# Two-layer decoder trunk on one core: order of the first loads, flags fetched one by one, later mixture weights, a second buffer of unsplit columns

## The chip, the core and the metric

The kernel runs on one core of a Trainium2 chip. The metric is the device time of one execution in microseconds (us), the median of several runs. The core's engines are TensorE (PE, its weight loads PEld), VectorE (DVE), ScalarE (ACT), GpSimd (POOL) and SyncE (SP). Each takes its own instructions in order; semaphores order them against each other. SP and ACT issue DMAs, and 16 DMA engines carry them.

## What is computed

A trunk of two layers on 256 tokens of width 1024, all in float32. Each layer is a token mixer and a feed-forward part, both with RMS norm, and both shifted, scaled and gated by columns that come from a vector c through a matrix ("ada"). The feed-forward part of layer 0 is dense, that of layer 1 a mixture of 8 experts, two for each token. Cut to what matters:

```python
mod = silu(c) @ ada_w[l] + ada_b[l]           # 6 x 1024: shift, scale, gate, twice
h = rms_norm(x, norm_mix[l]) * (1 + scale) + shift
x = x + gate * hybrid_mixer(h, ...)           # gated DeltaNet and stick-breaking attention
h = rms_norm(x, norm_ffn[l]) * (1 + scale2) + shift2
x = x + gate2 * (swiglu(h) if l == 0 else moe_swiglu(h))
# moe_swiglu: logits = h @ router_w + router_b; the two largest of 8; softmax over the two;
#   y_e = (silu(xb @ w1[e]) * (xb @ w3[e])) @ w2[e]; summed with the mixture weights
out = rms_norm(x, final_norm)
```

The width of an expert's hidden layer is 3584.

## The kernel before

**Stages.** Four stages follow each other: mixer 0 (to about 366 us, the program's start included), the dense feed-forward part (to 640), mixer 1 (to 996) and the experts (to 1965). Weights come from HBM in units of 1 MB on SP's queue. A unit is split into a high part (`CAST hl` on ACT) and a low part (`lo`, a subtraction on DVE), and a product is made of three matmuls of parts.

**Program start.** `ada_first` loads eight 1 MB units of ada_w (tiles `f`), makes silu(c) (tile `csil`, a column of 128 partitions by 8, loaded element by element, L145), spreads it (L235) and multiplies (L252). `setup(0)` loads five small tensors of rows on ACT's queue into the tile `rows` (L174 to L178), and PE turns them into columns (L183). `load_rows` loads the first constants `cst` (L157, the identity for transposes among them) and x (L158). The router's bias and matrix (`rb`, `rw`, L1112, L1113) and `setup(1)`'s five loads have no place of their own in the program: a scheduler puts them where their operands are free, which is on ACT's queue in these first 20 us. Each DMA reports to one of eight semaphores, taken in turn; a DMA waits for the landing of the one that had its semaphore before.

**Experts.** `route` finds each token's two experts, its slot with each, and the mixture weights `wt`. `Light` sets a flag for each expert with at most 64 tokens (`light`, `lighti`) and loads the eight flags into registers of PE (L1207, TENSOR_LOAD). By the flag a branch (`arms`) takes one of two ways for each pair of units: `few` multiplies the unsplit weights (L1372 up, L1454 down), `heavy` the parts (L1351 up, L1438 and L1443 down). `gather` builds selection matrices `pe` (L1214, L1215, L1296) and gathers two experts' tokens with 32 matmuls (L1314), whose columns ACT and DVE split (L1325, L1330, L1331). The experts' hidden layer is worked off in blocks of 1024 columns; `down` of a block runs after the next block's `up`. `turned` transposes the hidden columns (L1412) and copies them, split (`t2r`, L1416, L1417) and unsplit (`s`, L1420; one buffer, `s32`). `begin(e)` makes, at an expert's start, its mixture weights by slot (`ws`, L1393, L1402) and the matrix `pte` (L1398, L1400) that puts its rows back; `finish` uses both (L1488, L1493, L1494).

**Order.** A scheduler places instructions by priority and readiness; a DMA marked with `keep_in_program_order`, as those of the experts' weights on SP are, stays where the program has it.

Of the kernel before, what the change touches and what calls it, by code (L numbers as in the profile page):

```python
# [11 lines left out]
F32 = mybir.dt.float32  # L12
# [7 lines left out]
P = 128  # L20
# [53 lines left out]
def trunk_kernel(  # L74
# [17 lines left out]
    phase_b = dict(raw2=4, hl2=1, lo=4, r4=6, x32=3, s32=1, t2=5, t2r=6, gt=1, xn=2, pe=2, pte=2)  # L92
# [77 lines left out]
    def setup(l):  # L170

        rows = pc.tile([P, 2, P], F32, tag="rows", name=f"rows{l}")
        G.memset(rows, 0.0)
        nc.scalar.dma_start(rows[0:48, 0, :], ada_b[l].rearrange("(r p) -> r p", p=P))  # L174
        nc.scalar.dma_start(rows[48:56, 0, :], norm_mix[l].rearrange("(r p) -> r p", p=P))
        nc.scalar.dma_start(rows[56:64, 0, :], norm_ffn[l].rearrange("(r p) -> r p", p=P))
        nc.scalar.dma_start(rows[64:65, 0, :], dn_out_norm[l : l + 1, :])
        nc.scalar.dma_start(rows[0:96, 1, :], conv_w[l].rearrange("j (r p) -> (j r) p", p=P))  # L178
# [53 lines left out]
    def ada_first(l, mods):  # L232

        cs = mk("r4", [P, 4 * S])[:, : 32 * KC].rearrange("p (k c) -> p k c", c=32)
        V.tensor_copy(cs, csil.unsqueeze(2).broadcast_to([P, KC, 32]))  # L235
        banks = {m: [bank(t) for _ in range(2)] for m, t in zip(mods, "gs")}
        raws = {}
        for m in mods:
            for q in range(4):
                raws[m, q] = ada_load(l, m, q, "f8")  # L240
                if len(raws) == 2:
                    load_rows()
                if len(raws) == 5:
                    rest = setup(0)
        for m in mods:
# [862 lines left out]
    class Router:  # L1108


        def __init__(self, l, j):
            nc.scalar.dma_start(rb, router_b[j : j + 1, :].partition_broadcast(P))  # L1112
            nc.scalar.dma_start(rw[:, 0], router_w[j].rearrange("(k p) n -> p k n", p=P))  # L1113
# [44 lines left out]
    def route():  # L1158
# [21 lines left out]
        wgt = sm([P, 2, 2])  # L1180
        V.tensor_sub(wgt, m8[:, :, 0:2], m8[:, :, 0:1].broadcast_to([P, 2, 2]))
        A.activation(wgt, wgt, AF.Exp)
        den = sm([P, 2])
        V.tensor_reduce(den, wgt, AX.X, ALU.add)
        V.reciprocal(den, den)
        V.tensor_tensor(wgt, wgt, den.unsqueeze(2).broadcast_to([P, 2, 2]), ALU.mult)
        V.tensor_tensor(wt, eq, wgt[:, :, 0:1].broadcast_to([P, 2, NE]), ALU.mult)
        V.tensor_tensor(tmp, tmp, wgt[:, :, 1:2].broadcast_to([P, 2, NE]), ALU.mult)
        V.tensor_add(wt, wt, tmp)
        return oa, wt, pos, light  # L1190

    zero = pc.tile([P, P], F32R, tag="zero", name="zero")
    most = pc.tile([P, 1], F32, tag="most", name="most")
    mosti = pc.tile([P, 1], I32, tag="mosti", name="mosti")

    class Light:


        def __init__(self, cnt):
# [4 lines left out]
            self.back = pc.tile([P, NE], F32, tag="back", name="back")  # L1204
            V.tensor_scalar(self.back, self.flag, -float(P // 2), None, ALU.mult)
            self.regs = [
                nc.values_load(self.int[0:1, e : e + 1], engines=[mybir.EngineType.PE], min_val=0, max_val=1)  # L1207
                for e in range(NE)
            ]

        def slots(self, e):

            t = mk("t2", [P, 512])[:, 0:P]
            V.tensor_scalar(t, C["iota"], P // 2 - 0.5, self.back[:, e : e + 1], ALU.is_gt, ALU.mult)  # L1214
            V.tensor_add(t, t, C["iota"])  # L1215
            return t

# [6 lines left out]
    class Weights:  # L1224
# [53 lines left out]
        def group(self):  # L1278
# [5 lines left out]
    def experts(l, weights, xnh, xnl, oa, wt, pos, light, merge):  # L1284
# [50 lines left out]
        def up(e, n):  # L1335
# [8 lines left out]
            def heavy(u0, units):  # L1344
                for u, (_, hv, lv) in enumerate(units):
# [326 lines left out]
```

## Time and profile before

| | us |
|---|---|
| median of 3 runs | 1971.96 (1966.64 to 1973.22) |
| the profiled execution, its own time | 1972.13 |
| its span | 1970.3 |
| PE busy | 1823.6 (93%) |
| DVE busy | 1599.0 (81%) |
| ACT busy | 1283.3 (65%) |

The mean granted clock of TensorE was 0.965. The span runs from the first to the last recorded instruction; 1.8 us of the profiled execution's time lie around it. The chain of work that ended last is made of TensorE for 63%, DVE for 18%, ACT for 8% and DMA for 4%. In a timeline a row is one instruction or a run of alike ones: its start, its length, the engine, the line, what it writes and reads, and in brackets how long the engine was idle before it and what ended that. An engine with a q behind its name is its sequencer, which issues DMAs.

### The profile page before, as it was taken

The numbers are of one execution on the slowest core, as the hardware profiler recorded it, in microseconds if no ns is written. First come the engines' busy times: TensorE is split into PE (matmuls) and PEld (weight loads), VectorE is DVE, ScalarE is ACT, GpSimd is POOL, SyncE is SP. The second block draws the span as 40 slices with busy tenths as digits, with TensorE's granted clock in tenths as the row PEclk, the third lists the DMA queues.
The fourth block names the chain that finished last, engine by engine and source line by source line (L and its number), as shares of the span: only waits on it lengthen the run. The fifth ranks groups of instructions, "written<-read, shape, count | busy, mean of one in ns | idle before, by whom it ended". The sixth has DMA issues, their size and how long they took to land.

```text
span 1970.3 us, 36475 instructions
## 1 busy us (share of the span) xinstructions
PE 1823.6 (93%) x14868; PEld 1412.8 (72%) x14868; DVE 1599.0 (81%) x1900; ACT 1283.3 (65%) x1842; POOL 80.0 (4%) x88
## 2 busy tenths in 40 slices
PE   5899999999999899999979988999889998899986
PEld 2889989999999789989968733686337863378522
DVE  3778678687666878588668898997989889898998
ACT  2765556454443665556477788877788687886885
POOL 0101000000000101000000002000020001000000
PEclk8999999999999999999989999999899998899998
DMA  8544447688773344555739999999999999999995
GB/s 279 168 155 144 143 153 235 214 288 279 246 260 95 127 153 131 162 171 193 259 140 377 365 402 348 380 369 365 381 355 383 367 370 365 370 374 368 377 403 232
DMA packets 220334, 539.24 MB, mean 274 GB/s; under 512 B 13602, under 2 KB 120548, under 8 KB 206052
## 3 DMA queue, kind: packets, MB, share of 16 engines
q1 hardware_dynamic: 215216, 536.02, 74.7%
q8 instruction: 148, 2.42, 0.5%
q10 hardware_dynamic: 4916, 0.35, 0.2%
q14 instruction: 54, 0.44, 0.1%
HBM read 535.27 MB, written 1.06 MB: 272 GB/s over the span
## 4 chain that ended last, share of the span: by engine, by line
PE 63%; DVE 18%; ACT 8%; issue 7%; DMA 4%; DVEq 0%; SPq 0%; ACTq 0%
PE g L1351 15%; PE g L379 7%; PE g L375 7%; PE g L377 7%; DVE lo L1271 7%; PE a L1438 4%; PE g L1372 3%; ACT hl L1267 3%; DMA raw<-in_moe_w_dram 2%; PE a L1454 2%; PE a L1443 2%; DVE t L627 2%; DVE hl L340 2%; ACT hl L339 1%; PE a L1055 1%
## 5 line engine op out<-in xcount | busy, mean ns | idle before, releaser
L1271 DVE TENSOR_TENSOR lo<-raw,hl 128x2048 fp32r<-128x2048 f32 (+1 forms) x338 | 754.1, 2272 | 46.5 <-ACT hl L1267 46.4
L1267 ACT CAST hl<-raw 128x1024 fp32r<-128x1024 f32 x672 | 657.3, 1052 | 26.0 <-DMA raw<-in_moe_w_dram 21.6
L340 DVE TENSOR_TENSOR hl<-raw,hl 128x1024 fp32r<-128x1024 f32 (+1 forms) x252 | 298.1, 1188 | 136.8 <-ACT hl L339 136.4
L339 ACT CAST hl<-raw 128x1024 fp32r<-128x1024 f32 (+1 forms) x252 | 256.8, 1022 | 201.3 <-PE g L379 134.0
L375 PE MATMUL g<-r,hl 128*128 128x256 f32 x1536 | 235.2, 293 | 6.6 <-ACT r L483 3.4
L377 PE MATMUL g<-r,hl 128*128 128x256 f32 x1536 | 228.6, 288 | 0.0
L379 PE MATMUL g<-r,hl 128*128 128x256 f32 x1536 | 223.9, 287 | 0.4 <-DVE hl L340 0.4
L1351 PE MATMUL g<-hl,r 128*128 128x512 f32 x896 | 222.9, 391 | 0.0
L375 PEld LDWEIGHTS g<-r,hl 128*128 128x128 f32 x1536 | 204.2, 194 | 15.2 <-ACT r L483 4.7
L1372 PE MATMUL g<-raw,x 128*64 128x512 f32 (+1 forms) x1024 | 212.1, 563 | 0.0
L377 PEld LDWEIGHTS g<-r,hl 128*128 128x128 f32 x1536 | 204.6, 195 | 3.0 <-issue 2.5
L379 PEld LDWEIGHTS g<-r,hl 128*128 128x128 f32 x1536 | 202.6, 194 | 2.6 <-issue 1.9
L1351 PEld LDWEIGHTS g<-hl,r 128*128 128x128 f32 x896 | 167.4, 188 | 37.0 <-ACT hl L1267 2.4
L1372 PEld LDWEIGHTS g<-raw,x 128*64 128x64 f32 x1024 | 71.5, 141 | 114.6 <-issue 104.2
L1454 PE MATMUL a<-raw,s 128*64 128x512 f32 x448 | 120.2, 684 | 3.6 <-ACT s L1420 3.2
L1351 PE MATMUL g<-lo,r 128*128 128x512 f32 x448 | 120.7, 391 | 0.5
L1416 ACT CAST t2r<-a 128x512 fp32r<-128x512 f32 x56 | 32.8, 585 | 113.1 <-PE a L1412 113.1
L1351 PEld LDWEIGHTS g<-lo,r 128*128 128x128 f32 x448 | 83.6, 188 | 20.0 <-DVE lo L1271 2.9
L210 DVE SCALAR_TENSOR_TENSOR f<-raw,csil,f 128x1024 f32<-128x1024 f32 x70 | 92.5, 1322 | 5.7 <-DMA raw<-in_ada_w_dram 5.2
L1438 PE MATMUL a<-hl,t2r 128*128 128x512 f32 x224 | 89.0, 397 | 1.7 <-ACT hl L1267 1.7
L1454 PEld LDWEIGHTS a<-raw,s 128*64 128x64 f32 x448 | 34.3, 157 | 74.5 <-issue 67.3
L1443 PE MATMUL a<-hl,t2r 128*128 128x512 f32 x224 | 87.5, 390 | 0.0
(334 smaller groups left out, 2211.6 us busy)
## 6 DMA issues: line engine op xcount, KB each, us to landing
raw<-in_moe_w_dram SPq DMA_DIRECT2D x334, 1024.0 KB, 7.0
raw<-in_w_in_dram SPq DMA_DIRECT2D x60, 1024.0 KB, 5.4
raw<-in_ffn_w_dram SPq DMA_DIRECT2D x42, 1024.0 KB, 5.8
raw<-in_ada_w_dram SPq DMA_DIRECT2D x40, 1024.0 KB, 5.3
f<-in_ada_w_dram SPq DMA_DIRECT2D x8, 1024.0 KB, 8.6
raw<-in_w_up_dn_dram SPq DMA_DIRECT2D x8, 1024.0 KB, 5.1
raw<-in_w_out_dram SPq DMA_DIRECT2D x8, 1024.0 KB, 5.0
raw<-in_w_up_sb_dram SPq DMA_DIRECT2D x4, 1024.0 KB, 5.1
```

The costliest lines, as they stand in the source:

```text
L339: A.copy(hv, part)
L340: V.tensor_sub(lv, part, hv.bitcast(F32))
L375: T.matmul(pv[:, b, :], hv[:, k, :], xh[:, k, :], start=(k == 0), stop=False)
L377: T.matmul(pv[:, b, :], hv[:, k, :], xl[:, k, :], start=False, stop=False)
L379: T.matmul(pv[:, b, :], lv[:, k, :], xh[:, k, :], start=False, stop=(k == kc - 1))
L1267: A.copy(hi[:, h, :], raw[:, h, :])
L1271: V.tensor_sub(lo[:, h, :], raw[:, h, :], hi[:, h, :].bitcast(F32))
L1351: T.matmul(ps, x_[:, kk, :], w[:, k, 512 * b : 512 * b + 512], start=(kk == 0 and x_ is xh and w is hv), stop=(kk == KC - 1 and w is lv),)
L1372: T.matmul(banks[0][h, 0:half], x32[:, kk, :], w[:, k, half * i : half * i + half], start=(wide and kk == 0), stop=(kk == KC - 1), skip_gr ...
L1438: T.matmul(ye[nb], gh[:, gs], w[:, k, nw], start=(first and q == 0 and u == 0 and p == 0), stop=(last and u == 1 and p == 3),)
L1443: T.matmul(ye[nb], gl[:, gs], w[:, k, nw], start=False, stop=False)
L1454: T.matmul(ye[nb][h, :], g32[:, gs], w[:, k, 512 * nb : 512 * nb + 512], start=False, stop=(last and u == 1 and k == 1), skip_group_check= ...
```

## The change

- **First loads.** c is loaded as a row of 8 by 128 (`crow`), goes through Silu, and PE transposes it into `csil`. The first constants are first on SP's queue. The five row loads go into a tile of the ring `t2`. `setup(1)`'s five loads and the router's two are marked to stay in program order.
- **Flags.** `Light` no longer fetches eight registers; `fetch(e)` fetches one, called from `begin(e)`. A slot's fold is one operation of DVE with a precomputed `foldr` rather than two with `back`.
- **Mixture weights.** Their seven operations become `mix()`, called once after the first gather.
- **Unsplit columns.** `s32` has two buffers and `pte` one. `slots(e)` (the second half of the old `begin`) makes `ws` and `pte` just ahead of an expert's last `down`.
- **Arms.** `few` and `heavy` are written for one unit and called for the two of a pair; `group` is renamed `take`. Up to seven units rather than five are asked for at the experts' start.

```diff
-    phase_b = dict(raw2=4, hl2=1, lo=4, r4=6, x32=3, s32=1, t2=5, ... pe=2, pte=2)
+    phase_b = dict(raw2=4, hl2=1, lo=4, r4=6, x32=3, s32=2, t2=5, ... pe=2, pte=1)
...
-    nc.scalar.dma_start(csil, c_in[0].rearrange("(k p) -> p k", p=P))
-    A.activation(csil, csil, AF.Silu)
+    crow = pc.tile([KC, P], F32, tag="crow", name="crow")
+    nc.scalar.dma_start(crow, c_in[0].rearrange("(k p) -> k p", p=P))
+    A.activation(crow, crow, AF.Silu)
...
+    nc.sync.dma_start(cst[:, :first], cst_in[:, :first])
...
     def load_rows():
-        nc.sync.dma_start(cst[:, :first], cst_in[:, :first])
         nc.sync.dma_start(x, x_in[0].rearrange("(b p) d -> p b d", p=P))
...
-        rows = pc.tile([P, 2, P], F32, tag="rows", name=f"rows{l}")
+        pin = tc.keep_in_program_order if l else lambda ins: ins
+        rows = mk("t2", [P, 512])[:, 0 : 2 * P].rearrange("p (i c) -> p i c", c=P)
         G.memset(rows, 0.0)
-        nc.scalar.dma_start(rows[0:48, 0, :], ada_b[l].rearrange("(r p) -> r p", p=P))
+        pin(nc.scalar.dma_start(rows[0:48, 0, :], ada_b[l].rearrange("(r p) -> r p", p=P)))
...
-        V.tensor_copy(cs, csil.unsqueeze(2).broadcast_to([P, KC, 32]))
...
-                if len(raws) == 5:
+                if len(raws) == 4:
                     rest = setup(0)
+        ps = bank("a")
+        T.transpose(ps[:, 0:KC], crow, ident[0:KC, 0:KC])
+        V.tensor_copy(csil, ps[:, 0:KC])
+        V.tensor_copy(cs, csil.unsqueeze(2).broadcast_to([P, KC, 32]))
...
-            self.back = pc.tile([P, NE], F32, tag="back", name="back")
-            V.tensor_scalar(self.back, self.flag, -float(P // 2), None, ALU.mult)
-            self.regs = [
-                nc.values_load(self.int[0:1, e : e + 1], engines=[mybir.EngineType.PE], min_val=0, max_val=1)
-                for e in range(NE)
-            ]
+            self.regs = {}
...
-            V.tensor_scalar(t, C["iota"], P // 2 - 0.5, self.back[:, e : e + 1], ALU.is_gt, ALU.mult)
-            V.tensor_add(t, t, C["iota"])
+            V.scalar_tensor_tensor(t, foldr, self.flag[:, e : e + 1], C["iota"], ALU.mult, ALU.add)
...
         def begin(e):
+            light.fetch(e)
+            st[e] = []
+
+        def slots(e):
...
         drain([gather(0)])
+        merge.begin()
...
                 if late:
+                    if late[1:3] == blocks[-1]:
+                        ends = slots(late[0])
                     for _ in down(*late[:3], *g):
...
+        G.tensor_scalar(foldr, C["iota"], P // 2 - 0.5, -float(P // 2), ALU.is_gt, ALU.mult)
         with tc.high_priority(offset=0):
-            weights.load(5)
+            weights.load(7)
```

**Program start, ACT's queue.** Before, from the first DMA on; `rows` and `t` are tiles for small tensors.

```order
L145 DMA csil<-in_c_dram 128x8x1
L174 DMA rows_112<-in_ada_b_dram 48x128
L175 DMA rows_112<-in_norm_mix_dram 8x128
L176 DMA rows_112<-in_norm_ffn_dram 8x128
L177 DMA rows_112<-in_dn_out_norm_dram 1x128
L146 ACT_TABLE_LOAD
L146 ACTIVATE csil<-csil 128x8
L178 DMA rows_112<-in_conv_w_dram 96x128
L490 DMA t_15_159<-in_w_in_dram 128x8x16
L1112 DMA rb<-in_router_b_dram 128x8
L1113 DMA rw<-in_router_w_dram 128x8x8
L494 CAST hl_161<-t_15_159 128x8x16
```

The same stretch after.

```order
L146 DMA crow<-in_c_dram 8x128
L176 DMA t_10_111<-in_ada_b_dram 48x128
L177 DMA t_10_111<-in_norm_mix_dram 8x128
L178 DMA t_10_111<-in_norm_ffn_dram 8x128
L179 DMA t_10_111<-in_dn_out_norm_dram 1x128
L147 ACT_TABLE_LOAD
L147 ACTIVATE crow<-crow 8x128
L180 DMA t_10_111<-in_conv_w_dram 96x128
L495 DMA t_17_164<-in_w_in_dram 128x8x16
L499 CAST hl_166<-t_17_164 128x8x16
```

The load of c is now 8 rows of 128 rather than 128 by 8 single elements, and `rb` and `rw` have left this stretch; they now stand at mixer 1's start behind its `CAST hl<-t`. `setup(1)`'s five loads, which stood a few rows further down here, now stand at the feed-forward part's start, between its last `ACTIVATE r` and three `CAST hl`.

**Program start, SP's queue.** Before:

```order
L198 DMA f_6_100<-in_ada_w_dram 128x2x1024
L198 DMA f_7_102<-in_ada_w_dram 128x2x1024
L157 DMA cst<-in_cst_dram 128x160
L158 DMA x<-in_x_dram 128x2x1024
L198 DMA f_8_106<-in_ada_w_dram 128x2x1024
```

After, the first constants are first; their issue waited for the landing of `norm_mix` in the rows of the semaphores before, and waits for none after, where x waits for the landing of `ada_b`:

```order
L150 DMA cst<-in_cst_dram 128x160
L200 DMA f_6_102<-in_ada_w_dram 128x2x1024
L200 DMA f_7_104<-in_ada_w_dram 128x2x1024
L159 DMA x<-in_x_dram 128x2x1024
L200 DMA f_8_107<-in_ada_w_dram 128x2x1024
```

The rest of SP's start is in the same order: six more units of ada_w, the first of w_in, the rest of the constants.

**Start of the experts, PE.** Ahead of the first gather's 32 matmuls (L1314 before, L1322 after), before; of the eight register loads the last two are shown, each with two instructions of its sequencer:

```order
L1176 MATMUL a_12187<-rt,ones 128x8 x2
...
L1207 TENSOR_LOAD lighti
L1207 ISA x2
L1207 TENSOR_LOAD lighti
L1207 ISA x2
L1314 MATMUL a_12313<-pe_12296,xn_12288 128x256
```

After, there and at the gather's end:

```order
L1181 MATMUL a_12197<-rt,ones 128x8 x2
L1222 TENSOR_LOAD lighti
L1222 ISA x2
L1222 TENSOR_LOAD lighti
L1222 ISA x2
L1322 MATMUL a_12229<-pe_12214,xn_12206 128x256
...
L1322 MATMUL a_12283<-pe_12214,xn_12207 128x256
L1222 TENSOR_LOAD lighti
...
L1222 ISA x2
L1227 COMPARE_AND_BRANCH
```

Two loads stand ahead of the gather and six between it and the first branch; the four matmuls of L1393 and L1398, which stood between gather and branch, are gone from there.

**The last expert's end, ACT.** From the last transposed columns to the last branch, before and then after:

```order
L1416 CAST t2r_31600<-a_31595 128x512
L1267 CAST hl_31512<-raw_4465_31423 128x1024 x2
L1267 CAST hl_31550<-raw_4466_31425 128x1024 x2
L1219 UNCONDITIONAL_BRANCH
L1267 CAST hl_31556<-raw_4480_31503 128x1024 x2
L1420 COPY s_4492_31604<-a_31595 128x512
```

```order
L1429 CAST t2r_31577<-a_31572 128x512
L1275 CAST hl_31489<-raw_4465_31400 128x1024 x2
L1433 COPY s_4492_31581<-a_31572 128x512
L1275 CAST hl_31527<-raw_4466_31402 128x1024 x2
L1413 CAST pte_31588<-a_31583 128x256
L1227 UNCONDITIONAL_BRANCH
L1275 CAST hl_31533<-raw_4480_31480 128x1024 x2
```

The copy `s`, for which PE's last L1454 waits, moved ahead of four of the six casts, and `pte`'s cast came in between.

## Rows read from the trace of the kernel before

**Rows 1.** the page: the span, and the chain that ended last by engine.

```profile
span 1970.3 us, 36475 instructions
...
PE 63%; DVE 18%; ACT 8%; issue 7%; DMA 4%; DVEq 0%; SPq 0%; ACTq 0%
```

**Rows 2.** DMA over 0:60 us in 40 slices of 1.5 us: GB/s moved.

```profile
GB/s 0 156 336 261 375 294 2 121 284 348 168 413 265 10 197 380 404 399 399 421 415 423 403 358 350 403 169 226 360 367 197 132 183 338 188 0 85 333 295 3
```

**Rows 3.** waits of SP over 0:60 us: line, awaited work, total us, times, longest.

```profile
SPq L198 <- DMA rw<-in_router_w_dram: 8.6, 1, 8.6
SPq L157 <- DMA rows<-in_norm_mix_dram: 8.4, 1, 8.4
```

**Rows 4.** timeline of PE over 0:43 us: start, us, engine, line, work, idle before.

```profile
35.59 1.91 PE L252 MATMUL s<-f,r 128*32 128x512 f32 x8 [0.67 <-DMA f<-in_ada_w_dram]
...
42.00 1.41 PE L503 MATMUL a<-r,hl 128*128 128x256 f32 x5 [3.43 <-DVE t L484]
```

**Rows 5.** timeline of ACT over 0:45 us.

```profile
0.75 0.51 ACTq L145 DMA_DIRECT2D csil<-in_c_dram  x1
...
9.79 0.21 ACT L146 ACTIVATE csil<-csil 128x8 f32<-128x8 f32 x1 [5.37 <-DMA csil<-in_c_dram]
...
10.65 0.58 ACTq L1112 DMA_DIRECT2D rb<-in_router_b_dram  x1
11.28 0.45 ACTq L1113 DMA_DIRECT2D rw<-in_router_w_dram  x1
...
15.59 0.44 ACTq L176 DMA_DIRECT2D rows<-in_norm_ffn_dram  x1
17.43 0.23 ACTq L177 DMA_DIRECT2D rows<-in_dn_out_norm_dram  x1
```

**Rows 6.** timeline of the feed-forward part's start, 380:420 us.

```profile
394.89 1.07 ACT L339 CAST hl<-raw 128x1024 fp32r<-128x1024 f32 x1
...
396.07 2.04 ACT L339 CAST hl<-raw 128x1024 fp32r<-128x1024 f32 x2
396.25 1.06 PE L377 MATMUL g<-r,hl 128*128 128x256 f32 x4
```

**Rows 7.** timeline of ACT at mixer 1's start, 639:646 us.

```profile
643.34 2.84 ACT L483 ACTIVATE r<-a,mod,aw 128x256 fp32r<-128x256 f32 x6 [2.71 <-PE a L470]
```

**Rows 8.** timeline of the experts' start, 1000:1018 us.

```profile
1000.69 0.16 DVE L1203 CAST lighti<-light 128x8 int32<-128x8 f32 x1
...
1001.86 1.10 DVE L1296 TENSOR_SCALAR pe<-t,rt 128x128 fp32r<-128x128 f32 x4
...
1006.72 5.76 PE L1314 MATMUL a<-pe,xn 128*128 128x256 f32 x32 [6.51 <-issue]
1008.87 1.02 ACT L1325 ACTIVATE t<-a,mod,aw 128x256 f32<-128x256 f32 x2 [7.24 <-PE a L1314]
...
1012.86 2.08 PE L1351 MATMUL g<-hl,r 128*128 128x512 f32 x8
```

**Rows 9.** busy us of each engine by window, clock, DMA share, GB/s.

```profile
1039.00:1063.00 24.00, 24.00 (x111) 20.03 (x110) 20.70 (x13) 15.06 (x18) 0.00 (x0) 1.00 1.00 378
1183.00:1207.00 24.00, 21.50 (x106) 9.29 (x104) 20.82 (x18) 20.07 (x32) 7.86 (x6) 0.97 0.89 319
```

**Rows 10.** waits of ACT over 1017:1960 us.

```profile
ACT t2r L1416 <- PE a L1412: 113.1, 25, 7.3
...
ACT pte L1400 <- PE a L1398: 14.8, 7, 2.5
```

**Rows 11.** timeline of the experts' end, 1936:1971 us.

```profile
1946.35 6.83 DVE L1271 TENSOR_TENSOR lo<-raw,hl 128x2048 fp32r<-128x2048 f32 x5 [0.55 <-ACT hl L1267]
...
1950.01 0.58 ACT L1420 COPY s<-a 128x512 f32<-128x512 f32 x1
...
1950.64 3.65 PE L1454 MATMUL a<-raw,s 128*64 128x512 f32 x16 [3.25 <-ACT s L1420]
...
1954.33 1.41 DVE L1488 SCALAR_TENSOR_TENSOR t<-a,sm,gt 128x512 f32<-128x512 f32 x2 [1.14 <-PE a L1454]
```

More of the change, by code (lines that the diff above doesn't have):

```diff
@@ L1445, in few, with heavy @@
-            def few(q, units):
-                if first and q == 0:
+            def heavy(m, _, hv, lv):
+                (gh, gl), u = parts[m // 2], m % 2
+                for p, (k, w) in enumerate(((0, hv), (1, hv), (0, lv), (1, lv))):
+                    gs = slice((2 * u + k) * P, (2 * u + k + 1) * P)
+                    for nb in range(2):
+                        nw = slice(512 * nb, 512 * nb + 512)
+                        T.matmul(
+                            ye[nb], gh[:, gs], w[:, k, nw], start=(first and m == 0 and p == 0),
+                            stop=(last and m == n // 256 - 1 and p == 3),
+                        )
+                        if p < 2:
+                            T.matmul(ye[nb], gl[:, gs], w[:, k, nw], start=False, stop=False)
@@ L1447, in few @@
+            def few(m, w, *_):
+                if first and m == 0:
                     for nb in range(2):
                         T.matmul(ye[nb], zero, parts[0][0], start=True, stop=True, skip_group_check=True)
-                for u, (w, _, _) in enumerate(units):
-                    i, at = (q, u) if n > 512 else (u, 0)
-                    for k in range(2):
-                        gs = slice((2 * at + k) * P + i * HS, (2 * at + k) * P + i * HS + HS)
-                        for nb, h in enumerate(halves):
-                            T.matmul(
-                                ye[nb][h, :], g32[:, gs], w[:, k, 512 * nb : 512 * nb + 512],
-                                start=False, stop=(last and u == 1 and k == 1), skip_group_check=True,
-                            )
@@ L1459, in down @@
-            for q in range(n // 512):
-                units = weights.group()
-                light.arms(e, lambda: few(q, units), lambda: heavy(q, units))
+                i, at = divmod(m, n // 512)
+                for k in range(2):
+                    gs = slice((2 * at + k) * P + i * HS, (2 * at + k) * P + i * HS + HS)
+                    for nb, h in enumerate(halves):
+                        T.matmul(
+                            ye[nb][h, :], g32[:, gs], w[:, k, 512 * nb : 512 * nb + 512],
+                            start=False, stop=(last and m == n // 256 - 1 and k == 1), skip_group_check=True,
+                        )
@@ L1462, in down, with finish @@
+            for m0 in range(0, n // 256, 2):
+                units = weights.take()
+                light.arms(
+                    e, lambda: [few(m0 + i, *t) for i, t in enumerate(units)],
+                    lambda: [heavy(m0 + i, *t) for i, t in enumerate(units)],
+                )
                 weights.load(5)
                 yield
-        def finish(e):
-            pte, ws, ye = st.pop(e)
+        def finish(e, pte, ws):
+            ye = st.pop(e)
             ys = [mk("t2", [P, 512]) for _ in range(2)]
@@ L1544, in experts @@
         g = turned(late[3])
+        ends = slots(late[0])
         drain([down(*late[:3], *g)])
         merge.end()
-        finish_last(late[0])
+        finish_last(late[0], *ends)
     def moe(l, j, r):
@@ L1570, in moe, with begin @@
             gt = None
+            mixed = False
+            def begin(self):
+                if not self.mixed:
+                    self.mixed = True
+                    mix()
             def start(self):
```

120 lines of the change are left out of this document (57 added, 63 removed).

## The prediction, made before the changed kernel was run

> **What bounds the kernel now.** I read the page first: the span is 1970.3 us, and the chain that ended last is TensorE for 63%, DVE for 18% and DMA for only 4% [rows 1]. So one engine's total decides nothing; each stage has to be asked for itself what ends last there. Next come the places that the change touches: the program's start, the starts of the feed-forward part and of mixer 1, the experts' start, their body, and their end.
>
> At the program's start the reader is to see transfers that bound the work and have holes. The 1.5 us slices [rows 2] read 399 to 423 GB/s from 25 us on, but 2 GB/s at 9 us, 10 at 19.5 us, and mostly less than 350 between. The waits name both holes: SP stood 8.4 us until the row load of norm_mix had landed and 8.6 us until the router's matrix had landed [rows 3], each because the next large load shares that small load's semaphore. The load of c, 1024 single elements, was issued at 0.75 us; its use began at 9.79 us [rows 5]. PE's last products with ada_w wait for their unit (`<-DMA f`) and begin at 35.59 us; the mixer's first matmul follows at 42.00 us [rows 4]. What lies between is a fixed chain of small operations.
>
> At the experts' start PE waits 6.51 us with the reason "issue" ahead of the gather [rows 8]. `lighti` is written by 1000.85 us, so the eight register loads take (1006.72 − 1000.85) / 8 = 0.73 us each. The first branch's matmuls begin at 1012.86 us [rows 8]. In the body the DMA share is 1.00 in an ordinary window and 0.89 where a later gather runs [rows 9]: transfers bound it, and PE's or DVE's time is worth little there. The last expert's end is bound by DVE's splits and one wait of PE for the copy `s` [rows 11].
>
> **Program start.** The change removes the 1024-element load (8 rows instead), takes `rb`, `rw` and `setup(1)`'s five loads off this stretch, and puts the constants first. It adds one transpose, one small copy, and a wait of x for ada_b. Without the scattered load ahead of it, ada_b, issued second on ACT's queue, should land while the first two ada units still flow, so this wait should be covered; if it is not, SP holds x and six units behind it, and PE waits for these. What must move up to the last ada unit is 8 units and x of 1.049 MB each and 0.08 MB of constants, 9.52 MB. Before, the slices up to 34.5 us sum to 9.71 MB [rows 2], which agrees. After, I keep the first 9 us as they were (six slices, 1422 GB/s in sum times 1.5 us = 2.13 MB) and let the remaining 7.39 MB flow at 405 GB/s, the middle of the undisturbed slices: 18.2 us, so the end is at 27.2 us instead of 34.5 us. Gain **7.3 us**. Bounds: at 358 GB/s, one of the weaker slices among the good ones, 20.6 us and a gain of 4.9; with the full rate from 1.5 us on, 1.5 + 23.5 = 25.0 us and a gain of 9.5. Everything behind is a chain without clock time, so it shifts whole. PE's eight pairs of products fit: a unit's 8 matmuls take 1.91 us [rows 4] and a unit 2.6 us to come.
>
> A rule that speaks for the low end: the rows show 399 to 423 GB/s for ten slices [rows 2]. The Trainium skill, DMA: Bandwidth & Descriptors, section Specifications, gives about 358 GB/s as a core's limit from HBM. By it the end would lie at 9.0 + 20.6 = 29.6 us and the sum would give 2.4 us less gain. The trace is above that limit, so the measurement decides.
>
> **Feed-forward start.** The five row loads are now issued by ACT between its `ACTIVATE r` and three `CAST hl`. One such issue takes 0.23 to 0.44 us [rows 5], five 1.2 to 2.2 us. Queued behind them are the casts that ran at 394.89 and 396.07 us, and PE's L377 from 396.25 us waits for the first of these [rows 6]. Two copies of columns leave that place. PE has other matmuls for part of it, so I take **+0.6 us**, ends 0 and +2.2. The transposes that need these rows come about 100 matmuls later, more than the landing needs.
>
> **Mixer 1's start.** `rb` and `rw` cost ACT 0.58 + 0.45 = 1.03 us [rows 5], in front of an activation that waited 2.71 us for PE [rows 7]. Covered: **0**; without that cover 1.0.
>
> **Experts' start.** Two loads now stand ahead of the gather, six behind it. `pe` was done at 1002.96 us; without `back` and with one operation instead of two for a slot it is done near 1002.3 us, and two loads end at 1000.85 + 1.47 = 1002.3 us. The gather thus starts 4.4 us earlier, ends near 1008.1 us (5.76 us long), and six loads of 0.73 us bring the branch to **1012.5 us**, against 1012.86: only **−0.4 us**. The loads were moved, not removed. Ends: if loads run beside the matmuls, the branch still needs the high and low columns; ACT now casts unit 1 only behind the gather's first activations and DVE's low columns queue behind that unit's split (gather's first activation 2.15 us after the gather's start as before [rows 8], 1.5 us of activations, 2.0 of casts [rows 6], some 2.3 of split and 0.4 of the column), near 1011 us: −1.9. If register loads wait for the matmul queue to empty, +1.0.
>
> A rule against this part: the row gives 0.73 us a load with eight in a line [rows 8]. The Trainium skill, DMA: Bandwidth & Descriptors, section Latency and other measured facts, gives a load of a register from memory a floor of about 0.6 us, which grouping amortizes. By it six grouped loads cost an estimated 3.6 us or less and the sum would be 0.8 us better; the eight loads in the trace were grouped and still cost 0.73 each, so I keep the row.
>
> **Body.** `slots` saves about 0.5 us of DVE for each of three later gathers, where the DMA share dips [rows 9]; the second buffer of `s32` lets the copy run earlier. I take **−1.0**. Ends: nothing, or the dips filled: 0.11 of 24 us, 2.6 us, for each of three gathers, −7.9. On the loss side stands the rival below. Asking for seven units rather than five changes nothing that I can find: units six and seven were already issued ahead of the router.
>
> **Experts' end.** The copy `s` ran at 1950.01 us, behind six casts, and PE waited 3.25 us for it [rows 11]. It is now ahead of four of them, so PE's last L1454 can start some 3 us earlier. Next late is DVE: its splits run until 1946.35 + 6.83 = 1953.18 us [rows 11], and L1488 began at 1954.33. So **−0.9**, ends 0 (`pte`'s cast and the copy delay the last splits) and −1.1.
>
> Sum: −7.3 + 0.6 − 0.4 − 1.0 − 0.9 = −9.0 us. From the profiled execution's 1972.13 us, which is 0.2 us above the median of the runs, this gives 1963.1; I predict **1963 us**. A difference of 0.3%, 5.9 us, is about what a measurement of this kernel can tell from no change: faster means under 1966.0, slower above 1977.9.
>
> **Rivals.** (1) *The hole is only traded.* Small row loads still land late (a load of w_in in 64-byte pieces stays at the start), and x with six units behind it waits for ada_b as cst waited for norm_mix. Half the gain, 3.7 us, and the full feed-forward cost of 2.2: −3.7 + 2.2 − 0.4 − 1.0 − 0.9 = −3.8, 1968.3 us: no change. For it: a wait of exactly this form stood there, 8.4 us. Against it: the slow load ahead of it is gone.
>
> (2) *The gathers fill.* With copies and slots out of the way the three dips go: −9.0 − 6.9 = −15.9, 1956 us. Against it: the dip is PE waiting on the gather itself, which stays.
>
> (3) *Slower.* `pte` has one buffer now, and its cast stands in ACT's order ahead of the casts of the last `down`'s units. It waited 14.8 us over 7 times before, while the neighbouring `t2r` waited 113.1 us over 25, 4.5 each [rows 10]. If `pte`'s wait grows to 7.3 us, the longest of these, from 14.8 / 7 = 2.1, ACT stands 5.2 us more for each of eight experts. ACT has 24 − 20.1 = 3.9 us free in a window of 24 [rows 9], spread over it; if half of that covers the wait, 3.2 us are left, 26 us in all, which hold splits, and so raw buffers and transfers: −9 + 26 = +17, 1989 us. From an uncovered 1.1 us for each expert it eats the gain, and from 1.9 us the kernel is slower by more than the bound. For it: transfers bound the body and have no slack to catch up. Against it: two PE matmuls and two transposes are ready early.
>
> (4) *Not what it says.* The flags are not read one at a time at each expert: the order shows all eight ahead of the first branch. That is in the sum (−0.4) already.
>
> **How the numbers follow.** Forecast 0.62; rival 1 0.20; rival 2 0.10; rival 3 0.08. The forecast's own bounds give about 1958 (full rate at the start, better branch) to 1967 (358 GB/s, 2.2 us of issues). The range takes in rival 1 and the edge of rival 2: 1956 to 1970. Faster: forecast and rival 2, 0.72; within 0.3%: 0.20; slower: 0.08.
>
> **What would show it.** Start: no slice under 100 GB/s between 3 and 25 us, SP's waits on norm_mix and rw gone, the last ada matmuls at about 28.3 us and the mixer's first matmul near 34.7. Feed-forward start: at most 2 us lost on PE. Experts' start: the gather 4.4 us earlier, "issue" idle behind it of about 4.4 us, the branch 0.4 us earlier. Body: DMA share as before. End: L1488 about 1 us earlier relative to DVE's last split, PE's wait for `s` gone. Wrong would be a new wait of SP of several us at the start, a branch that starts later than before relative to `lighti`, or body windows with a DMA share below 0.96 where it was 1.00.

## The result, and the profile after

The changed kernel takes 1954.76 us (median of 4 runs, 1951.51 to 1955.75) against 1971.3 us (4 runs, 1966.64 to 1973.22): a ratio of 0.9917, 95% interval 0.9895 to 0.9938. It is faster by 16.5 us where 9 were forecast, and lies 1.2 us below the lower end of the range. The direction was right, the size was not. One execution of the changed kernel in a later group (a_again, below) took 4418 us and is left out of every median here.

The profiled execution is the fastest of the four (1951.51 us). The page, with the lines that answer to [rows 1]:
```profile
span 1949.6 us, 36491 instructions
...
PE 62%; DVE 17%; ACT 10%; issue 6%; DMA 4%; SPq 1%; ACTq 0%; DVEq 0%
```

The span is 20.7 us shorter, 4 us more than the medians say. The table cuts both profiled executions at the same places of the trace (the mixers and the feed-forward part from PE's or ACT's first row in them, the experts' body from the first heavy matmul to the issue of the last weights, their end from there to DVE's first L1488 or L1502). Each column is one execution.

| stretch | before, us | after, us | difference | forecast |
|---|---|---|---|---|
| start, to mixer 0's first matmul | 42.0 | 34.6 | -7.4 | -7.3 |
| mixer 0 | 346.1 | 348.0 | +1.9 | 0 |
| feed-forward part | 255.3 | 255.1 | -0.2 | +0.6 |
| mixer 1 and router, to the writing of the flags | 357.1 | 355.3 | -1.8 | 0 |
| flags to the first heavy matmul | 12.4 | 9.8 | -2.6 | -0.4 |
| experts' body | 924.4 | 912.7 | -11.7 | -1.0 |
| experts' end | 17.1 | 18.1 | +1.0 | -0.9 |

**The start.** The 1.5 us slices, against [rows 2]: the holes at 9 and 19.5 us are gone.
```profile
GB/s 0 117 330 366 412 352 309 413 407 418 407 407 415 404 410 412 404 411 358 355 382 275 350 348 350 147 0 137 353 209 0 74 319 309 14 0 0 0 5 5
```

SP's waits there, against [rows 3] (line, awaited work, total us, times, longest). The waits for norm_mix and the router are gone; a smaller one for ada_b and one for a small load of w_in stand in their place.

```profile
SPq L159 <- DMA t<-in_ada_b_dram: 3.7, 1, 3.7
SPq L329 <- DMA t<-in_w_in_dram: 2.3, 1, 2.3
```

PE, against [rows 4], and then ACT, against [rows 5] (start, us, engine, line, work, idle before). c is used at 4.04 us instead of 9.79, and the last ada products and the mixer's first matmul come 7.4 us earlier. ACT now waits 10.58 us for the small load of w_in, with the sums of squares of x (L416) behind that.

```profile
28.19 1.91 PE L257 MATMUL s<-f,r 128*32 128x512 f32 x8 [0.69 <-DMA f<-in_ada_w_dram]
...
34.61 1.58 PE L508 MATMUL a<-r,hl 128*128 128x256 f32 x7 [3.44 <-DVE t L489]
```

```profile
4.04 0.31 ACT L147 ACTIVATE crow<-crow 8x128 f32<-8x128 f32 x1
14.92 0.30 ACT L499 CAST hl<-t 128x128 fp32r<-128x128 f32 x1 [10.58 <-DMA t<-in_w_in_dram]
...
15.37 0.64 ACT L416 ACTIVATE t<-x 128x512 f32<-128x512 f32 x1
```

**The experts' start**, against [rows 8]:

```profile
993.23 0.15 DVE L1212 CAST lighti<-light 128x8 int32<-128x8 f32 x1
...
995.13 6.59 PE L1322 MATMUL a<-pe,xn 128*128 128x256 f32 x32 [2.36 <-DVE mosti L1601]
...
997.28 1.02 ACT L1333 ACTIVATE t<-a,mod,aw 128x256 f32<-128x256 f32 x2 [4.05 <-PE a L1322]
...
1002.85 0.73 PE L1358 MATMUL g<-hl,r 128*128 128x512 f32 x2 [1.12 <-ACT t L1333]
...
1004.18 2.43 PE L1358 MATMUL g<-hl,r 128*128 128x512 f32 x5 [0.60 <-DVE r L1339]
```

The gather starts 1.75 us behind the flags' writing instead of 5.87: two loads of 0.73 us and 0.3 us more. (Its row names `mosti`, written just before; but with three loads ahead, in b_flags below, the gather starts 2.47 us behind the flags.) The first heavy matmul starts 7.7 us behind the gather's start. The six register loads between them (line, sequencer, operation, count: ns least/median/most, first and last start):

```profile
L1222 PEldq TENSOR_LOAD <-lighti x6: 298/300/312, 998.3 to 1001.7; - x6
```

They do not wait for the gather's end at 1001.72 us: the first starts 3.15 us behind the gather's start, while PE is still at it, and the six run on at a pitch of 0.69 us ((1001.71 - 998.28) / 5) to 1002.4. The branch's first matmul follows 0.45 us later. Its row names ACT's `t` for the wait, but the experiment on the flags' loads, below, shows the loads to be last. So some 3.4 us of the loads lie beside matmuls, where the forecast had put all 4.4 behind them.

**The body.** DVE's and ACT's waits from five us behind the first heavy matmul to the last weights' issue, first of the kernel before:

```profile
DVE lo L1271 <- ACT hl L1267: 45.8, 46, 2.3
```

```profile
ACT t L1325 <- PE a L1314: 11.8, 6, 2.2
ACT s L1420 <- DVE t2r L1417: 9.6, 7, 1.4
```

And after:

```profile
DVE lo L1279 <- ACT hl L1275: 32.2, 48, 1.8
```

```profile
ACT t2r L1429 <- PE a L1425: 116.8, 24, 7.5
...
ACT s L1433 <- DVE t2r L1430: 16.7, 10, 2.6
```

Two of ACT's rows of before are gone altogether: `pte`'s 14.8 us [rows 10] and the 11.8 us for the gathers' first columns (L1325). `s` waits 16.7 us instead of 9.6, and DVE waits 13.6 us less for ACT's casts. The whole body as one window (busy us of PE, PEld, DVE, ACT and POOL, granted clock, DMA share, GB/s), before and then after:

```profile
1012.86:1937.24 924.38, 863.50 (x3890) 541.37 (x3891) 846.49 (x556) 735.10 (x881) 31.86 (x29) 0.96 0.98 372
```

```profile
1002.85:1915.54 912.69, 856.40 (x3894) 541.41 (x3896) 847.88 (x552) 734.61 (x880) 26.02 (x30) 0.97 0.98 377
```

The mean DMA share is 0.98 in both. Had the 11.7 us been dips that filled, it would have risen to 0.99 (0.98 x 924.4 / 912.7); instead the same bytes moved at 377 GB/s rather than 372.

**The end**, by a window of before and two of after (columns as above) and by PE's and DVE's timeline after, against [rows 11]. Before:

```profile
1946.00:1952.00 6.00, 2.75 (x16) 0.73 (x14) 5.65 (x5) 4.59 (x6) 0.00 (x0) 1.00 0.09 36
```

and after:

```profile
1920.00:1926.00 6.00, 4.09 (x16) 2.34 (x18) 5.40 (x5) 3.43 (x6) 0.00 (x0) 0.71 0.70 281
1926.00:1932.00 6.00, 6.00 (x22) 1.79 (x20) 6.00 (x5) 3.76 (x5) 0.00 (x0) 0.72 0.01 5
```

```profile
1923.81 9.80 PE L1465 MATMUL a<-raw,s 128*64 128x512 f32 x32
```
```profile
1933.64 1.41 DVE L1502 SCALAR_TENSOR_TENSOR t<-a,sm,gt 128x512 f32<-128x512 f32 x2 [1.49 <-PE a L1465]
```

PE's wait for `s` is gone. But the granted clock is 0.71 and 0.72 in these windows, against 1.00 before, and 32 matmuls of L1465 take 9.80 us, where 16 took 3.65 [rows 11].

### The profile page after: what moved, and what is told of

It reads as the page before. It is cut to its first block, busy times and chain, and to the rows that moved or that the text cites. A ratio compares the mean times of both kernels' runs of the same rounds, so it can differ in the third digit from the quotient of the medians.

```text
span 1949.6 us, 36491 instructions
## 1 busy us (share of the span) xinstructions
PE 1815.0 (93%) x14869; PEld 1410.4 (72%) x14869; DVE 1598.0 (82%) x1892; ACT 1283.1 (66%) x1842; POOL 75.8 (4%) x89
## 4 chain that ended last, share of the span: by engine, by line
PE 62%; DVE 17%; ACT 10%; issue 6%; DMA 4%; SPq 1%; ACTq 0%; DVEq 0%
PE g L1358 16%; PE g L380 7%; PE g L384 7%; PE g L382 7%; DVE lo L1279 5%; PE a L1450 5%; ACT hl L1275 3%; DMA raw<-in_moe_w_dram 3%; PE a L1455 2%; PE a L1465 2%; DVE t L632 2%; DVE hl L345 2%; PE g L1378 1%; ACT hl L344 1%; PE a L1060 1%
## 5 line engine op out<-in xcount | busy, mean ns | idle before, releaser
L1378 PE MATMUL g<-raw,x 128*64 128x512 f32 (+1 forms) x1024 | 208.0, 550 | 0.0
L1465 PE MATMUL a<-raw,s 128*64 128x512 f32 x448 | 115.4, 663 | 0.8 <-DMA raw<-in_moe_w_dram 0.8
L1465 PEld LDWEIGHTS a<-raw,s 128*64 128x64 f32 x448 | 33.6, 152 | 68.4 <-issue 64.8
```

The lines of the kernel that those rows point to most:

```text
L1378: T.matmul(banks[0][h, 0:half], x32[:, kk, :], w[:, k, half * i : half * i + half], start=(wide and kk == 0), stop=(kk == KC - 1), skip_gr ...
L1465: T.matmul(ye[nb][h, :], g32[:, gs], w[:, k, 512 * nb : 512 * nb + 512], start=False, stop=(last and m == n // 256 - 1 and k == 1), skip_g ...
```

## Experiments

The runs of a group shared one chip and its runs of the kernel before. Names that begin with b are made from the kernel before, those with a from the changed one; n marks kernels cut behind mixer 1. The question behind the first eight: which part brings the body's 11.7 us, and is it ACT's in-order wait for `pte` (theory A), or rather the second buffer, DVE's shorter `slots`, or PE's work that left the experts' starts.

### One part alone

b_start is the new program start in the kernel before (the first hunks of the diff, with the router's pins). b_flags only fetches the flags in `begin`:

```diff
-            self.regs = [
-                nc.values_load(self.int[0:1, e : e + 1], engines=[mybir.EngineType.PE], min_val=0, max_val=1)
-                for e in range(NE)
-            ]
+            self.regs = {}
...
+            light.fetch(e)
```

b_slots only moves `slots`:

```diff
-    phase_b = dict(... s32=1, ... pte=2)
+    phase_b = dict(... s32=1, ... pte=1)
...
         def begin(e):
+            st[e] = []
+
+        def slots(e):
...
-            st[e] = (pte, ws, [])
+            return pte, ws
...
                 if late:
+                    if late[1:3] == blocks[-1]:
+                        ends = slots(late[0])
```

and b_slots_s32 adds `s32=2` to that.

> The kernel before with the program's first loads of the changed kernel alone (row load of c, constants first, setup(1)'s and the router's loads pinned). Both theories of the body expect the same here: the mixer's first matmul about 7.4 us earlier than at 42.0 us, and the body (from the first heavy matmul, L1351, to L1488) as long as before, 941 us, so about 1964 us in all, ratio 0.996. Had the body's gain come from the start (transfers in another phase) or from the run, the body would be shorter here too: about 930 us, ratio 0.991.

> The kernel before with the flags fetched one by one alone: three register loads ahead of the first gather, five behind it. If loads run beside matmuls that PE has already been handed, the first heavy matmul comes about 2 to 2.6 us earlier relative to the writing of lighti (before 12.17 us behind it) and the rest is as before: 1969 us. If each load waits until the matmuls are done, it comes at most 0.4 us earlier.

> The kernel before with ws and pte of an expert made just ahead of its last down, pte with one buffer, nothing else. Theory A (ACT's seven waits for L1398, 14.8 us, and PE's extra matmuls at each expert's start held the splits): the body is 5 to 10 us shorter, 931 to 936 us, ACT's wait for pte near 0, DVE's wait for ACT's casts down from 45.8 us to about 33; 1962 to 1966 us in all. Theory B (the second buffer of the unsplit columns): within 1 us of before, 1971.

> As the one with the slots moved, and the unsplit columns with two buffers. Theory A: as without the second buffer, within 2 us. Theory B: 7 to 10 us faster than with the slots moved alone; body about 931 us.

| kernel | median us (before 1969.38) | ratio, 95% interval | start | flags to heavy | body | 
|---|---|---|---|---|---|
| b_start | 1966.38 | 0.9986 (0.9973 to 0.9999) | 35.9 | 12.5 | 923.8 |
| b_flags | 1968.69 | 0.9998 (0.9989 to 1.0007) | 41.8 | 10.7 | 921.4 |
| b_slots | 1961.82 | 0.996 (0.9946 to 0.9973) | 41.9 | 12.2 | 915.4 |
| b_slots_s32 | 1955.8 | 0.9932 (0.9918 to 0.9946) | 42.6 | 12.4 | 914.1 |

The last three columns are of the profiled executions. The body's gain comes with the moved slots: 9 us of body alone, 7.6 us of time. (b_flags leaves the body as it was, and its 921.4 is 3.0 us below 924.4: so much do single executions differ.) DVE's and ACT's waits with the slots alone moved:

```profile
DVE lo L1271 <- ACT hl L1267: 38.7, 38, 4.0
```
```profile
ACT t2r L1419 <- PE a L1415: 117.9, 24, 7.5
...
ACT t L1325 <- PE a L1314: 14.8, 6, 3.5
```

`pte` has left ACT's list; the wait for the gathers' columns (L1325) is still there. It went with the second buffer, which adds 6 us of time by the medians and 1.3 us of body by the profiled executions; the expectations were within 2 or 7 to 10. In b_flags the first heavy matmul comes 10.5 us behind the writing of `lighti` instead of 12.2, 1.7 us earlier, where 2 to 2.6 or at most 0.4 were expected; the time shows nothing. The start alone was worth 3.0 us, not 6.1 as the mixer's first matmul of its own profiled execution says: the expectation of 1964 us was missed on the weak side.

### The changed kernel again, and without a part

a_again is the changed kernel. a_s32_1 has `s32=1` in place of 2. a_nostart takes the start back but for `setup`'s loads:

```diff
-    nc.scalar.dma_start(crow, c_in[0].rearrange("(k p) -> k p", p=P))
-    A.activation(crow, crow, AF.Silu)
+    nc.scalar.dma_start(csil, c_in[0].rearrange("(k p) -> p k", p=P))
+    A.activation(csil, csil, AF.Silu)
...
-    nc.sync.dma_start(cst[:, :first], cst_in[:, :first])
...
+        nc.sync.dma_start(cst[:, :first], cst_in[:, :first])
...
-            tc.keep_in_program_order(nc.scalar.dma_start(rb, router_b[j : j + 1, :].partition_broadcast(P)))
+            nc.scalar.dma_start(rb, router_b[j : j + 1, :].partition_broadcast(P))
```

b_nocast is the kernel before, which leaves out seven of `pte`'s eight casts: the later experts' rows are put back with the first expert's matrix.

```diff
-            pte = mk("pte", [P, S], F32R)
-            A.copy(pte, ps[:, 0:S])
+            if e == 0:
+                once.append(mk("pte", [P, S], F32R))
+                A.copy(once[0], ps[:, 0:S])
+            pte = once[0]
```

> The changed kernel once more, beside its variants. Both theories: 1953 to 1956 us, first matmul of mixer 0 at 34.6 us, body (first heavy matmul to the last weights' issue) 912 to 914 us, the granted clock's dip in mixer 0 in the same place or not: if it comes again, the order of the start causes it.

> The changed kernel with the old program start (element load of c, constants behind two ada units, rb and rw at the start). If the start is worth what the mixer's first matmul shows, 6 to 7.5 us slower than the changed kernel, about 1961 us, first matmul of mixer 0 near 41 to 42 us. If the gain is given back later, as the runs of the start alone suggest (0.9986), only 3 us slower, about 1957.5.

> The changed kernel with one buffer for the unsplit columns. If the second buffer is worth the difference of the two runs with moved slots: 4 to 6 us slower, 1959 to 1961, PE waiting again 7 to 9 us for DVE's t2r ahead of the three later gathers and ACT 12 to 15 us for the gathers' first columns. If that difference was only spread of the runs: within 2 us.

> The kernel before with pte cast for the first expert only, so that the later experts put their rows back with the first one's matrix; PE still makes the matrix and DVE still copies ws at every expert's start. Theory A (ACT's in-order wait for that cast holds the weights' splits): as the kernel with the slots moved, ratio 0.996 to before, body some 8 us shorter. Theory C (PE's four matmuls and DVE's copy at an expert's start are what costs): within 2 us of before.

| kernel | median us (before 1970.4) | ratio, 95% interval | start | body |
|---|---|---|---|---|
| a_again | 1951.78 | 0.9917 (0.9898 to 0.9937) | 35.1 | 914.5 |
| a_nostart | 1955.24 | 0.9923 (0.9909 to 0.9937) | 40.2 | 916.0 |
| a_s32_1 | 1956.06 | 0.9926 (0.9906 to 0.9945) | 38.0 | 914.9 |
| b_nocast | 1964.56 | 0.9971 (0.996 to 0.9982) | 42.1 | 915.6 |

b_nocast decides for theory A: leaving out seven casts of 0.37 us, 2.6 us of ACT's work, brings 5.8 us of time and nearly the same body as the moved slots, 915.6 us, although PE's four matmuls and DVE's copy are still at each expert's start. The casts' own work is too little for that, and in the kernel before nobody but DVE's copy of `ws` (0.3 us) waited for a cast's end at an expert's start; what costs is ACT's stand ahead of them. DVE's row shows the way to the weights' splits:

```profile
DVE lo L1271 <- ACT hl L1267: 35.4, 39, 3.5
```

How the splits then speed the transfers is argued, not shown: in b_slots and b_nocast too the body's mean DMA share is 0.98, at 375 GB/s. With one buffer again, ACT's wait for the gathers' columns is back in a_s32_1:

```profile
ACT t L1333 <- PE a L1322: 15.2, 6, 3.6
```

The second buffer is worth 4.3 us by the medians here, as expected (4 to 6), but 0.4 us of body by the profiled executions, and the two kernels' runs overlap; that it frees the gathers is shown, its size is not settled (between 0.4 and 6 us). The start is again worth half by the medians, 3.5 us, while the first matmuls lie 5.1 us apart. And a_s32_1, with the same start as a_again, begins its mixer 2.9 us later. So the start itself was open.

### The start without the experts

These kernels write x out behind mixer 1 and leave the experts and the final norm out:

```diff
         router.end(rms)
+    nc.sync.dma_start(out[0].rearrange("(b p) d -> p b d", p=P), x)
+    return
     with phase("e1", ...
```

n_crow is n_before with the row load of c and its transpose alone.

> The kernel before up to the end of mixer 1: the experts and the final norm are left out and x is written out, so that the spread of the experts' transfers is gone. About 1000 us; it is the base for the two runs beside it.

> The changed kernel cut in the same way. If the start keeps what the first matmul of mixer 0 shows in the profiled executions: 6 to 7.5 us faster than the cut kernel before. If half is given back before the experts: about 3 us.

> The kernel before, cut in the same way, with the row load of c and its transpose alone; the constants stay behind two ada units, and rb, rw and setup(1)'s loads stay at the start. If the scattered load of c is the cause of the first hole (SP's wait for norm_mix): half of the gain or more, 3 to 5 us against the cut kernel before. If the other small loads are the cause: under 1.5 us.

n_before takes 997.72 us (996.31 to 998.68), n_after 994.65 (993.43 to 996.3), n_crow 993.5 (993.1 to 994.05). The new start is worth 3.1 us, and the row load alone 4.2: by the medians everything else in the start together costs 1.1 us, though the two kernels' runs overlap. In n_after's profiled execution the first matmul of the mixer comes at 39.33 us, 4.7 us later than in the whole changed kernel with the same start. ACT's rows there, and PE's:

```profile
20.09 0.30 ACT L499 CAST hl<-t 128x128 fp32r<-128x128 f32 x1 [15.76 <-DMA t<-in_w_in_dram]
...
20.54 0.64 ACT L416 ACTIVATE t<-x 128x512 f32<-128x512 f32 x1
```

```profile
25.99 0.47 PE L475 MATMUL v<-cst,f 128*128 128x128 f32 x1 [5.57 <-DVE f L451]
...
30.46 3.77 PE L257 MATMUL s<-f,r 128*32 128x512 f32 x32
...
39.33 1.84 PE L508 MATMUL a<-r,hl 128*128 128x256 f32 x7 [3.44 <-DVE t L489]
```

The 64 KB load of w_in, in 1024 pieces of 64 bytes on ACT's queue, landed 17 us after its issue, between the ada units; ACT stood 15.76 us at its cast, the sums of squares came 5.2 us later than in the changed kernel's own profile, PE waited 5.57 us for the normed x, and the second half of the ada products stood behind that on PE. The landing differs from execution to execution, and the mixer's first matmul with it:

| kernel, all with the new start | cast of that load begins, us | mixer 0's first matmul, us |
|---|---|---|
| a_twice (below) | 12.94 | 34.5 |
| after | 14.92 | 34.6 |
| a_again | 14.77 | 35.1 |
| b_start | 17.08 | 35.9 |
| a_s32_1 | 19.02 | 38.0 |
| n_after | 20.09 | 39.3 |

With the cast at 13 to 15 us the mixer begins at 34.5 to 35.1; behind that its start moves with the cast. Hence theory D: in the timed executions this cast, through ACT's order, takes back half of what the new start gives.

### That cast held back

n_late and a_late are n_after and the changed kernel with one edit: the cast may be issued only behind the last sum of squares.

```diff
-        wba = narrow_weights(w_in[0][:, C_BA : C_BA + 16], 16)
+        wba_raw = narrow_load(w_in[0][:, C_BA : C_BA + 16], 16)
...
-                sumsq(b, slice(512 * h, 512 * h + 512), h)
+                seen = sumsq(b, slice(512 * h, 512 * h + 512), h)
         xn = unit_rows(2)
+        wba = narrow_split(wba_raw, 16, seen)
...
-        A.copy(wv[:, :, 0:n], raw)
+        with tc.issue_after(seen.ins) if seen else nullcontext():
+            A.copy(wv[:, :, 0:n], raw)
```

> The changed kernel up to the end of mixer 1 (experts and final norm left out), with ACT's cast of the 64 KB load of w_in held until the four sums of squares are done. Theory D (the load in 64-byte pieces lands 12 to 17 us after its issue behind the ada units, ACT stands at its cast, and the norm of x and with it PE's in-order products come late): first matmul of mixer 0 near 34.5 us instead of 39.3, and 990 to 991 us against 994.65 of the cut changed kernel. Theory E (the start's gain is lost later, to the clock or the transfers of mixer 0): 994 to 995 us.

> The whole changed kernel with the same cast held. Theory D: 3 to 4 us faster than the changed kernel in timed runs, 1949 to 1950.5 us. Theory E: within 1.5 us of it, 1951.5 to 1954.5.

n_late takes 990.98 us (987.9 to 992.18): 3.7 us less than n_after and 6.7 less than n_before. It ran on another chip than these two, whose kernel before has a median 1.55 us lower; I estimate some 0.8 us of that for half a kernel, so about 3 us are left. Theory D holds for the cut kernel. ACT and PE of its profiled execution:

```profile
13.75 0.64 ACT L416 ACTIVATE t<-x 128x512 f32<-128x512 f32 x1
...
20.21 0.30 ACT L506 CAST hl<-t 128x128 fp32r<-128x128 f32 x1 [3.90 <-DMA t<-in_w_in_dram]
```

```profile
22.91 2.85 PE L257 MATMUL s<-f,r 128*32 128x512 f32 x16
...
35.41 1.18 PE L515 MATMUL a<-r,hl 128*128 128x256 f32 x7 [3.44 <-DVE t L489]
```

The load lands just as late (20.2 us), but nothing that the mixer's start needs stands behind it: the sums begin at 13.75 us, the second half of the ada products at 22.91 instead of 30.46, and the first matmul of the mixer comes at 35.41 us, where 34.5 was expected.

a_late takes 1951.3 us (1947.82 to 1954.51), ratio 0.9902 (0.9885 to 0.9919): the lowest median of all kernels here, but 0.5 us below a_again's where 3 to 4 were expected, on another chip, and the intervals overlap. (By the ratios, each to its own chip's kernel before, 0.9902 against 0.9917, it would be 3 us.) In the whole kernel theory D is thus not shown; the cut kernels resolve what the whole one can't.

### The flags' loads twice

a_twice fetches each flag twice:

```diff
         def fetch(self, e):
-            self.regs[e] = nc.values_load(
+            for _ in range(2):
+                self.regs[e] = nc.values_load(
```

> The changed kernel with every flag fetched twice: 2 register loads ahead of the first gather and 14 fetches less those 2, 12 or more, behind it, so 6 and more loads of 0.73 us are added. If a load waits until the matmuls ahead of it are done, the first heavy matmul comes 4.4 us or more later (gather to first heavy matmul 12 us instead of 7.7). If loads run while the matmuls handed out before them are still at work, the first 4.4 us stay hidden as in the changed kernel and only the excess shows: 12 loads are 8.8 us from the moment the last gather matmul is handed out, so 9 to 10 us from the gather's start.

The loads between gather and first branch, and PE's rows:

```profile
L1223 PEldq TENSOR_LOAD <-lighti x9: 296/302/312, 996.6 to 1002.1; - x9
```

```profile
993.42 6.72 PE L1323 MATMUL a<-pe,xn 128*128 128x256 f32 x32 [2.37 <-DVE mosti L1602]
1003.20 3.52 PE L1359 MATMUL g<-hl,r 128*128 128x512 f32 x8 [3.05 <-ACT r L1339]
```

The trace shows where the sixteen stand: 2 ahead of the gather, 9 between it and the first branch, and 5 behind the first pair of units, so the 12 of the expectation were 9. The nine again start 3.15 us behind the gather's start (996.57 - 993.42) and run at 0.69 us each to 1002.76. The first heavy matmul comes 0.44 us behind that and 9.8 us behind the gather's start, 2.1 us more than with six: three loads of 0.69. So the loads start beside the matmuls, but from there each one counts. In time nothing shows: 1954.23 us, ratio 0.9918 (0.9903 to 0.9932).

## Why the forecast was off

- **Body: the step that failed.** Forecast -1.0, measured -11.7 in the profiled executions (-9.9 in a_again's) and -7.6 us of time for the moved slots alone. I looked for DVE's saved operations and the gathers' dips. ACT's seven waits for `pte`, 14.8 us, stood in [rows 10], but I read them only as a danger (rival 3: the wait might grow) and never as a term that the change removes. By the same argument that priced the rival (ACT's casts hold the splits, these the buffers and the transfers) their end had to be a gain: 14.8 us at most, and 5.8 (b_nocast) to 7.6 (b_slots) came. Rival 3's mechanism was thus right and its sign wrong; `pte` makes no wait at all where it now stands. The bound of -7.9, made from the dips, covered the 7.6 by chance only: the share did not rise as filled dips would have it.
- **The second buffer** was in the same term without a price. It takes away the 11.8 us of ACT's waits for the gathers' columns; 0.4 to 6 us, not settled.
- **Experts' start: mis-sized.** Forecast -0.4, measured -2.6. I took the six loads as a row of work behind the matmuls. They start beside them, half-way through the gather, and the loads' end still opens the branch (0.43 to 0.45 us behind it in the changed kernel, a_twice and b_flags). My other end, "if loads run beside the matmuls", was priced at -1.9 with ACT's and DVE's columns as the next limit. These are next indeed: PE waits 0.60 us for DVE's `r` two matmuls behind the branch, so without the last loads little more would have come. The Trainium skill's floor for a register load of about 0.6 us (DMA: Bandwidth & Descriptors, section Latency and other measured facts) is close to the 0.69 of six in a row and does not explain the miss: the price of a load was nearly right, its place was wrong.
- **Start: right in the profile, half in the time.** Forecast -7.3, -7.4 in the profiled execution, 3.0 to 3.5 us by the timed runs that isolate it. Rival 1 named the load in 64-byte pieces, but let it hold SP's queue through ada_b; it held ACT, and through ACT's order x's norm and PE. Eleven slices in a row read 404 to 418 GB/s (of the kernel before, seven in a row read 399 to 423, not ten as I wrote). That is above the limit of about 358 of the Trainium skill (DMA: Bandwidth & Descriptors, section Specifications), the rule that spoke for the low end. In the cut kernel a wait ate the gain, not the rate: with the cast held it keeps 6.7 us. In the whole kernel the cause of the missing half stays open.
- **Feed-forward start: the cost did not come.** Forecast +0.6; the part is 0.2 us shorter, so the five issues were covered.
- **End: the mechanism was right, the clock hid it.** L1465 no longer waits. Where the granted clock stayed at 1.00 (a_again, a_twice) the end takes 16.2 and 16.1 us, 0.9 and 1.0 less than before, as forecast; in the changed kernel's profiled execution the clock fell and it takes 18.1. The old end does the same: 17.1 us at 1.00, but 18.0 in b_start and b_flags at a mean of 0.91.
- **Mixers, forecast 0:** neither difference belongs to the change. Mixer 0 takes 344.3 to 348.0 us in executions of the changed kernel, on both sides of the 346.1 before, and goes with the clock (last section). Mixer 1 takes 357.1 us before at a mean clock of 0.98 and 355.3 after at 0.99; in a_twice, with the change, it takes 357.9 at 0.98.
- **The sum.** By the medians, what was isolated is 3.0 (start) + 0.7 (flags) + 7.6 (slots) + 6.0 (second buffer) = 17.3 us, or 15.6 with a_s32_1's 4.3 for the buffer, against 16.5 measured; the parts' own spread is 1 to 3 us each, so the agreement is no proof of the parts.

## What to carry to other kernels

A wait that stands in the rows and that the change moves is a term of the sum on both sides: price its end before its growth. Where one resource bounds a stage (here transfers at a mean share of 0.98), follow the in-order engines whose work frees its buffers: 2.6 us of ACT's casts were worth 6 us, because seven waits stood with them. A gain at a program's start has to be followed through every in-order queue that small loads stand in, and a kernel cut behind the place resolves 3 us where the whole one can't.

## What the runs showed of the hardware

- **Register loads run beside matmuls that stand ahead of them.** Behind a gather of 32 matmuls (6.6 us) they started 3.15 us after its start in two kernels (in b_flags, behind a gather and six small matmuls, 3.96 us), and then took 0.69 us each, one after another.
- **A small load behind large ones lands late and unevenly.** 64 KB in 64-byte pieces, issued at about 3 us, landed 10 to 17 us later between 1 MB units in eight profiled executions, although it goes through another engine's queue. Issued at 9.8 us, with the old start (a_nostart), it landed 3.3 us later.
- **The granted clock goes with 2 to 4 us of a stage between executions.** In mixer 0 of the changed kernel, behind 1.56 and 0.93 us of idle PE, the granted clock fell to 0.50 (the lower of the two levels, 1.2 GHz), and 8 matmuls took 2.08 us where a_twice's took 1.21. In a_twice PE was idle for the same 1.56 and 0.93 us in front of that stretch, but it ran at 1.00, and the mixer took 344.3 us instead of 348.0. It is not the order of the start: the clock fell at this place in a_again (0.52 over 76 to 83 us), but also in a_nostart with the old start (0.50 over 82 to 88 us), whose mixers took 347.2 and 347.4 us. The runs don't show what decides. The windows and PE's rows of the changed kernel, then a window and a row of a_twice:

```profile
77.00:80.00 3.00, 3.00 (x26) 2.55 (x25) 1.19 (x7) 2.78 (x12) 0.00 (x0) 0.50 0.98 344
80.00:83.00 3.00, 3.00 (x17) 3.00 (x16) 2.32 (x4) 0.13 (x1) 0.00 (x0) 0.55 0.82 284
```

```profile
74.73 0.65 PE L682 MATMUL v<-cst,f 128*128 128x128 f32 x4 [1.56 <-ACT f L527]
76.31 1.11 PE L648 MATMUL v<-cst,t 128*128 128x128 f32 x4 [0.93 <-ACT f L683]
77.36 1.12 PE L746 MATMUL a<-f 128*64 128x64 f32 x16
78.41 2.08 PE L380 MATMUL g<-r,hl 128*128 128x256 f32 x8
```

```profile
77.00:80.00 3.00, 3.00 (x37) 2.76 (x36) 1.11 (x7) 3.00 (x13) 0.00 (x0) 1.00 0.99 345
```

```profile
77.92 1.21 PE L380 MATMUL g<-r,hl 128*128 128x256 f32 x8
```
